# Input blocks of a hybrid decoder layer: both token tiles of the first and last unit side by side, and the gate weights one unit sooner

## The chip, the cores and the metric

The kernel is one program on 1 core of one Trainium2 chip. The metric is device microseconds (us) of one execution; lower is better. The engines are TensorE (PE; PEld is its weight load), VectorE (DVE), ScalarE (ACT), GpSimd (POOL) and SyncE (SP), which here issues nearly all DMAs, in order.

## The reference

One layer on 2048 tokens of width 1024, all in fp32:

```python
h = rmsnorm(x, norm_w)
u, z_s, q, k, v, z_a = split(h @ w_in)             # six blocks of 512 columns
y_s = s5_branch(u, ...)                            # complex diagonal state space, scan over tokens, half-GLU
y_s = y_s * silu(z_s)
y_a = diff_attention(rope(rmsnorm(q)), rope(rmsnorm(k)), v, ...)   # 4 heads, two maps each, causal
y_a = y_a * silu(z_a)
x = x + concat([y_s, y_a]) @ w_out
gate = sigmoid(x @ ple_w_gate)
x = x + gate * (p @ ple_w_proj)
```

## The kernel before

**Precision.** Each large product is made of three TensorE passes over operands split in a high and a low part (`passes`: high by high, high by low, low by high). In the trace the parts are `wh`/`wl` for weights and `xh`/`xl` for tokens. So a tile of 128 tokens by 512 columns takes 8 rows of weights (128 of the 1024 inputs each) by 3 passes, 24 matmuls into one PSUM bank.

**Stage 1, the input products** (to about 710 us). The 2048 tokens are two halves, and a half is four units of 256 tokens, t = 0 to 3, each of two tiles of 128 tokens, j = 0 and 1. `blocks` lists the work: u of the second half and of the first, then k, zs, v, q, za of the first half, then zs, k, v, q, za of the second. u and zs are made with the weights as the stationary operand (line 778, `pmm` in pieces of 256 tokens). q, k, v and za are made with the tokens as the stationary operand (line 824, `pmm` of 128 tokens by 512 columns): the code writes all 8 rows for j = 0 and then all 8 rows for j = 1.

The weights come through `Streamer` `ws`, a ring of 8 rows (`WB`). A row is one DMA of 256 KB into `wraw` (three such buffers, `WRB`), a scaled copy on ACT to `wh` (line 282) and the rest on DVE to `wl` (line 283). `ws.release()` gives back one row and has the next one loaded; it is called behind the last use of the row, so in the last unit of a block, behind the row's matmuls for j = 1. The next block needs its rows from its first unit on. `KOUT = (0, 3)` names the first and the last unit; for zs they are already written row by row (line 762).

A tile of q or k leaves PSUM through a chain: square on ACT (line 842), sums on DVE (844), three small steps on POOL (845 to 847), the scaling on DVE (850), which is the last reader of the bank, then rotation on DVE, four transposes on PE into `ptr` (865) and two reads of `ptr` (867, 868). `ps_mm`, the pool of `pmm`, has four banks.

Between the units, `background` puts in pieces of the state-space branch: tables and 32 groups one behind the other (lines 507 to 656, `U`, `tab`, `parg`, `na`, `zz`, `pss`), and the half-GLU (`g...`, lines 676 to 719). It uses all engines. The program's order is not that of the code: a scheduler with a time model of its own orders the instructions of each engine when the program is built, and each engine then runs its list in order.

**Stage 2, attention** (about 710 to 1158 us), 4 heads by 8 units, with the first half of the output product (`half`) put in between.

**Stage 3a, the second half of the output product** (to about 1234 us): eight units t = 0 to 7. A unit's result is added on DVE to `x1`. Units 0 to 2 (`EOP = 3`) use one PSUM bank, `pmf`, 12 matmuls at a time, each time added by line 1185; from t = 3 on there are seven more banks (`pm`, line 1189). In this stage `gate_w` also prepares the gate weights: for each of four row pairs k it loads two tiles `wgr` (line 1161, two buffers), forms seven sums and differences (line 1154, `wgt`) and splits each in high and low (ACT line 1149, POOL or DVE line 1150, `wg`). One `next(gw)` is half of a k. `GWS` says how many halves follow the code of unit t: `{3: 2, 4: 2, 5: 3, 6: 1}`. Ahead of each load POOL copies a column of the previous unit's `x1` into `wgr` (line 1160), so that the load cannot start before that unit is done.

**Stage 3b, the gate** (from about 1250 us to the end): seven products per pair of units (line 1262, `pg`), from `oph`/`opl`, made of `x1` by ACT and POOL (lines 1235, 1236), and `wg`; PLE products (1278), and the output.

Of the kernel before, what the change touches and what calls it, by code (L numbers as in the profile page):

```python
# [11 lines left out]
F32 = mybir.dt.float32  # L12
# [52 lines left out]
KOUT = (0, 3)  # L65
WB = 8
ACB = 3
EOP = 3
GWS = {3: 2, 4: 2, 5: 3, 6: 1}
XEB = 14  # L70
RA3 = 2
SSE = 0
# [46 lines left out]
def hymba_kernel(ctx, tc, x_t, p_t, positions, norm_w, w_in, lam_re, lam_im, log_dt, b_re, b_im,  # L119
# [3 lines left out]
    V, A, G, T = nc.vector, nc.scalar, nc.gpsimd, nc.tensor  # L123
# [74 lines left out]
    with ExitStack() as p1:  # L198
# [7 lines left out]
        ps_mm = p1.enter_context(tc.tile_pool(name="ps_mm", bufs=4, space=PSUM))  # L206
# [69 lines left out]
        def build_w(c0, k):  # L276
            def make():
                raw = pr.tile([128, 512], F32, name="wraw", bufs=WRB)
                nc.sync.dma_start(raw, win[k * 128:(k + 1) * 128, c0:c0 + 512])
                wh = pw.tile([128, 512], F32R, name="wh")  # L280
                wl = pw.tile([128, 512], F32R, name="wl")
                A.activation(wh, raw, AF.Copy, scale=nw[:, k:k + 1])  # L282
                V.scalar_tensor_tensor(wl, raw, nw[:, k:k + 1], wh.bitcast(F32), op0=ALU.mult, op1=ALU.subtract)  # L283
                return wh, wl
            return make
# [8 lines left out]
        ws = Streamer([build_w(c0, k) for _, _, c0 in blocks for k in range(8)], WB)  # L294
# [438 lines left out]
        passes = ((0, 0), (0, 1), (1, 0))  # L733
        ude = None
        xi = 0
        for bi, (hf, kind, c0) in enumerate(blocks):
            leaving = bi == len(blocks) - 1 or blocks[bi + 1][0] != hf
            for t in range(4):
                tok = hf * HALF + t * 256
                xt = xs.get(xi + t)  # L740
                last_t = t == 3
                if kind == "zs" and t == 0:
                    norm_cols(hf)
                if kind in ("u", "zs"):
                    if kind == "u" and t == 0:
                        ude = [pg1.tile([128, L, 128], F32, name="stg") for _ in range(4)]
                    if bi == 0 and t < 2:

                        if t == 0:
                            first = [pool.tile([128, 512], F32, name=nm)[:, :256] for pool, nm, n in  # L750
                                     ((ps_mm, "pmm", 4), (ps_ss, "pss", 3), (ps_tr, "ptr", 1)) for _ in range(n)]
                            for k in range(8):
                                w = ws.get(k)
                                for t_ in range(2):
                                    for cb in range(4):
                                        for n, (a_, b_) in enumerate(passes):
                                            T.matmul(first[t_ * 4 + cb], lhsT=w[b_][:, cb * 128:cb * 128 + 128],
                                                     rhs=xs.get(t_)[a_][:, k, :],
                                                     start=(k == 0 and n == 0), stop=(k == 7 and n == 2))
# [6 lines left out]
                    else:  # L766
                        pms = [ps_mm.tile([128, 512], F32, name="pmm") for _ in range(2)]
                        pos_ = [pms[cb // 2][:, (cb % 2) * 256:(cb % 2) * 256 + 256] for cb in range(4)]
                        order = [(cb, k) for cb in range(4) for k in range(8)]
                    for cb, k in order:  # L770
# [3 lines left out]
                        pm = pos_[cb]  # L774
                        w = ws.get(bi * 8 + k)
                        if bi > 0 or t > 1:
                            for n, (a_, b_) in enumerate(passes):
                                T.matmul(pm, lhsT=w[b_][:, cb * 128:cb * 128 + 128], rhs=xt[a_][:, k, :],  # L778
                                         start=(k == 0 and n == 0), stop=(k == 7 and n == 2))
# [34 lines left out]
                else:  # L814
                    if kind in ("q", "k"):
                        sh_ = pg1.tile([128, H, 256], F32R, name="stg")
                        sl_ = pg1.tile([128, H, 256], F32R, name="stg")
                    for j in range(2):
                        ti = (tok // 128) + j
                        pm = ps_mm.tile([128, 512], F32, name="pmm")  # L820
                        for k in range(8):
                            w = ws.get(bi * 8 + k)
                            for n, (a_, b_) in enumerate(passes):
                                T.matmul(pm, lhsT=xt[a_][:, k, j * 128:j * 128 + 128], rhs=w[b_],  # L824
                                         start=(k == 0 and n == 0), stop=(k == 7 and n == 2))
                            if last_t and j == 1:
                                ws.release()
                        rows = slice(ti * 128, ti * 128 + 128)
                        if kind == "v":
                            vo = pt.tile([128, 512], F32, name="t2")  # L830
# [103 lines left out]
    with ExitStack() as p2:  # L934
# [90 lines left out]
        for h in range(H):  # L1025
# [6 lines left out]
            for i in ORD[h]:  # L1032
# [6 lines left out]
                for qt in range(2):  # L1039
                    tq = slice(qt * 128, qt * 128 + 128)  # L1040
                    n = t0 + qt * 128 + 128
# [15 lines left out]
                    for ci, cl in enumerate(chunks):  # L1057
                        end = 640 if ci == len(chunks) - 1 else 512
                        pi, o = where[ci]
                        for m in range(2):  # L1060
                            pss = ps_s.tile([128, 512], F32, name="pss2")
                            for e in range(2):
                                T.matmul(pss[:, :cl], lhsT=qd[:, e, m, tq], rhs=ks[m][:, c0:c0 + cl],  # L1063
                                         start=e == 0, stop=e == 1)
# [26 lines left out]
                    for kg in range(0, len(blocks_), 4):  # L1091
# [6 lines left out]
                        for k in range(nk):  # L1098
                            T.matmul(po[:, 0:128], lhsT=wt[:, k, :], rhs=vt[:, kg + k, :],  # L1099
                                     start=kg + k == 0, stop=kg + k == len(blocks_) - 1)  # L1100
# [23 lines left out]
    with ExitStack() as p3:  # L1124
# [12 lines left out]
        with ExitStack() as p3a:  # L1137
# [38 lines left out]
            for t, i in enumerate(order):  # L1176
# [4 lines left out]
                for n0 in range(0, 8, 2):  # L1181
# [5 lines left out]
                    pm = ps3.tile([128, 2, 256], F32, name="pm3")  # L1187
# [4 lines left out]
                else:  # L1192
                    kept.append(x1)
                for _ in range(GWS.get(t, 0)):
                    next(gw)
# [200 lines left out]
```

## Time and profile before

| | us |
|---|---|
| median of 3 runs (lowest, highest) | 1471.44 (1465.84, 1471.6) |
| profiled execution, its own time | 1468.54 |
| span of the profiled execution | 1466.8 |
| PE busy in the span | 1389.2 (95%) |
| DVE busy | 1067.0 (73%) |
| ACT, POOL busy | 768.0 (52%), 522.4 (36%) |
| PE idle before its first gate product | 15.4 |

The span is what the profile shows of one execution; 1.7 us lie around it. A busy share is a mean over all stages. A row of the waits names who waited for whom, how long in all, how often and the longest. In a row of a timeline, `[3.98 <-DVE wl L283]` says that the engine was idle for 3.98 us before that instruction, and that DVE's `wl` of line 283 came last of what it waited for.

### The profile page before, as it was taken

To read this page: it belongs to the slowest core of one execution; us is meant where nothing else is said; L and a number is where in the kernel's file an instruction comes from. 1 tells how busy PE (TensorE), PEld (TensorE's weight loads), DVE (VectorE), ACT (ScalarE), POOL (GpSimd) and SP (SyncE) were. 2 spreads that over 40 slices of the span, in tenths; PEclk is the share of its full clock that TensorE was granted. 3 is DMA by queue.
4 is the path that set the end of the run, shared out by engine and by line. 5 is a ranking of instruction groups with operands and counts; after the bars stand their busy time and mean duration, and the time that the engine had idled before them with its cause. 6 is when DMAs were issued, how large, how long until landed. Compare 5 with 4: busy or idle time off the path is not lost.

```text
span 1466.8 us, 27419 instructions
## 1 busy us (share of the span) xinstructions
PE 1389.2 (95%) x9602; PEld 1279.5 (87%) x9602; DVE 1067.0 (73%) x2527; ACT 768.0 (52%) x1689; POOL 522.4 (36%) x670
## 2 busy tenths in 40 slices
PE   7999899999899999999899999999999996999998
PEld 7998798778698878888699999988989896899998
DVE  8568788789898866774687767767887248656754
ACT  8543335456554545553577677777787213332231
POOL 6632410043010411340255455544335334543440
PEclk9999899999999999999999999999999998899999
DMA  7448666546755287556854644644443455132221
GB/s 244 131 127 263 200 190 210 159 125 211 237 179 177 94 232 185 150 168 203 255 145 125 181 127 119 177 127 152 116 144 122 153 189 205 58 116 76 70 80 58
DMA packets 219410, 230.34 MB, mean 157 GB/s; under 512 B 62712, under 2 KB 168328, under 8 KB 216712
## 3 DMA queue, kind: packets, MB, share of 16 engines
q1 hardware_dynamic: 216968, 224.40, 49.8%
q10 hardware_dynamic: 2304, 4.20, 0.8%
q8 instruction: 75, 1.23, 0.3%
q14 instruction: 63, 0.52, 0.1%
HBM read 152.19 MB, written 84.72 MB: 162 GB/s over the span
## 4 chain that ended last, share of the span: by engine, by line
PE 48%; DVE 19%; DMA 15%; ACT 6%; issue 6%; POOL 5%; SPq 2%; ACTq 0%; DVEq 0%; POOLq 0%
PE pg L1262 11%; PE pmf L928 7%; PE po L1099 7%; PE pss L1063 7%; PE ptw L1095 3%; PE pl L1278 3%; DMA wraw<-in_w_in_dram 3%; PE pmm L824 2%; PE pss L707 2%; PE pmm L778 2%; POOL qst L846 2%; DMA tab_scr<-tx 2%; DVE wl L283 2%; PE pm L928 2%; DVE zz L644 1%
## 5 line engine op out<-in xcount | busy, mean ns | idle before, releaser
L824 PE MATMUL pmm<-wh,xh 128*128 128x512 f32 x512 | 197.6, 395 | 7.0 <-ACT wh L282 6.6
L824 PE MATMUL pmm<-wl,xh 128*128 128x512 f32 x512 | 200.8, 395 | 2.1 <-DVE wl L283 2.1
L824 PE MATMUL pmm<-wh,xl 128*128 128x512 f32 x512 | 200.2, 393 | 0.0
L1063 PE MATMUL pss<-ks,qd 128*128 128x512 f32 (+3 forms) x640 | 185.1, 387 | 7.5 <-DVE st L1065 4.0
L1074 ACT ACTIVATE s<-s,st 128x1024 f32<-128x1024 f32 (+4 forms) x192 | 171.5, 897 | 37.3 <-DVE st L1065 32.8
L1262 PE MATMUL pg<-oph,wg 128*128 128x256 f32 x896 | 164.1, 286 | 15.4 <-ACT oph L1235 15.4
L1262 PEld LDWEIGHTS pg<-oph,wg 128*128 128x128 f32 x896 | 141.6, 195 | 15.6 <-ACT oph L1235 15.6
L1099 PE MATMUL po<-vt,wt 128*128 128x128 f32 x1088 | 152.3, 276 | 2.9 <-ACT yo L1111 1.5
L1099 PEld LDWEIGHTS po<-vt,wt 128*128 128x128 f32 x1088 | 142.2, 192 | 11.2 <-ACT wt L1097 3.2
L1065 DVE CUSTOM_DVE_ANT_0 s<-pss,mk,st 128x512 f32<-128x512 f32 (+2 forms) x192 | 122.1, 651 | 23.3 <-PE pss L1063 21.7
L778 PE MATMUL pmm<-xh,wl 128*128 128x256 f32 x448 | 128.9, 291 | 4.1 <-DVE wl L283 4.1
L778 PE MATMUL pmm<-xh,wh 128*128 128x256 f32 x448 | 124.9, 294 | 6.0 <-DVE stg L788 3.2
L778 PE MATMUL pmm<-xl,wh 128*128 128x256 f32 x448 | 128.5, 290 | 0.0
L1262 PE MATMUL pg<-opl,wg 128*128 128x256 f32 x448 | 127.2, 285 | 0.3 <-POOL opl L1236 0.3
L824 PEld LDWEIGHTS pmm<-wh,xh 128*128 128x128 f32 x512 | 96.2, 189 | 27.6 <-ACT wh L282 8.7
L1063 PEld LDWEIGHTS pss<-ks,qd 128*128 128x128 f32 x640 | 100.8, 192 | 17.5 <-DVE st L1065 8.0
L824 PEld LDWEIGHTS pmm<-wl,xh 128*128 128x128 f32 x512 | 96.6, 189 | 21.1 <-DVE wl L283 3.0
L824 PEld LDWEIGHTS pmm<-wh,xl 128*128 128x128 f32 x512 | 96.7, 189 | 18.2
L928 PE MATMUL pmf<-yh,woh 128*128 128x256 f32 x352 | 105.0, 298 | 4.5 <-DVE x L1185 3.6
L596 POOL TENSOR_TENSOR U<-U,rl 128x256 f32<-128x256 f32 x32 | 28.3, 884 | 220.5 <-DMA U<-ug_scr 169.5
L1065 DVE CUSTOM_DVE_ANT_0 s<-pss,mk 128x512 f32<-128x512 f32 (+3 forms) x128 | 78.5, 629 | 31.2 <-PE pss L1063 26.7
L928 PE MATMUL pmf<-yl,woh 128*128 128x256 f32 x352 | 99.8, 284 | 0.0
(385 smaller groups left out, 3906.1 us busy)
## 6 DMA issues: line engine op xcount, KB each, us to landing
wraw<-in_w_in_dram SPq DMA_DIRECT2D x96, 256.0 KB
xraw<-in_x_t_dram SPq DMA_DIRECT2D x40, 256.0 KB
tab<-tab_scr SPq DMA_DIRECT2D x64, 136.0 KB
qd<-qh_scr SPq DMA_DIRECT2D x64, 128.0 KB
qd<-ql_scr SPq DMA_DIRECT2D x64, 128.0 KB
xr<-in_x_t_dram SPq DMA_DIRECT2D x32, 256.0 KB
yin<-yt_scr SPq DMA_DIRECT2D x16, 512.0 KB
xp_scr<-xp SPq DMA_DIRECT2D x32, 256.0 KB
```

What stands on the lines that cost most here:

```text
L283: V.scalar_tensor_tensor(wl, raw, nw[:, k:k + 1], wh.bitcast(F32), op0=ALU.mult, op1=ALU.subtract)
L707: T.matmul(pm[:, e, :], lhsT=a_[:, k, m * 128:m * 128 + 128], rhs=b_[k], start=(k == 0 and n == 0), stop=(k == 3 and n == 2))
L778: T.matmul(pm, lhsT=w[b_][:, cb * 128:cb * 128 + 128], rhs=xt[a_][:, k, :], start=(k == 0 and n == 0), stop=(k == 7 and n == 2))
L824: T.matmul(pm, lhsT=xt[a_][:, k, j * 128:j * 128 + 128], rhs=w[b_], start=(k == 0 and n == 0), stop=(k == 7 and n == 2))
L928: T.matmul(pm[:, e, :], lhsT=w[k][b_][:, ms], rhs=y[a_][:, k, :], start=(k == 0 and n == 0), stop=(k == 3 and n == 2))
L1063: T.matmul(pss[:, :cl], lhsT=qd[:, e, m, tq], rhs=ks[m][:, c0:c0 + cl], start=e == 0, stop=e == 1)
L1065: V.tensor_tensor_reduce(sr[m][pi][:, o:o + cl], pss[:, :cl], mk[:, end - cl:end], scale=1.0, scalar=3.4e38 if ci == 0 else st[:, 2 * ci - ...
L1074: A.activation(sr[m][pi][:, :cl], sr[m][pi][:, :cl], AF.Exp, bias=st[:, ci + m:ci + m + 1], scale=-1.0, accum_out=st[:, 12 + 2 * pi + m:13 ...
L1095: T.transpose(ptw[:, k, :], blocks_[kg + k], ident)
L1099: T.matmul(po[:, 0:128], lhsT=wt[:, k, :], rhs=vt[:, kg + k, :], start=kg + k == 0, stop=kg + k == len(blocks_) - 1)
L1262: T.matmul(banks[mp][:, e], lhsT=wg[n][k][b_][:, m * 128:m * 128 + 128], rhs=x_[a_][:, k], start=k == 0 and q == 0, stop=k == 3 and q == 2)
L1278: T.matmul(banks[mp][:, e], lhsT=wp[k][b_][:, m * 128:m * 128 + 128], rhs=p_[a_][:, k], start=(k == 0 and q == 0), stop=(k == 1 and q == 2))
```

## The change

Two edits. In blocks k, v, q and za the first and the last unit (`KOUT`) now take two banks at once and go through the weights row by row, three matmuls for j = 0 and three for j = 1 of each row; in the last unit the row is given back right behind these six. What follows a tile (its way out of PSUM) is the same code, behind both tiles. And `GWS` becomes `{2: 2, 3: 2, 4: 2, 5: 2}`: each k of the gate weights stands whole behind one unit, the first behind unit 2. The number of matmuls and of all other operations is the same.

```diff
-GWS = {3: 2, 4: 2, 5: 3, 6: 1}
+GWS = {2: 2, 3: 2, 4: 2, 5: 2}
...
+                    both = t in KOUT
+                    for j, k in [(j, k) for k in range(8) for j in range(2)] if both else []:
+                        if k == 0:
+                            pms = (pms if j else []) + [ps_mm.tile([128, 512], F32, name="pmm")]
+                        w = ws.get(bi * 8 + k)
+                        for n, (a_, b_) in enumerate(passes):
+                            T.matmul(pms[j], lhsT=xt[a_][:, k, j * 128:j * 128 + 128], rhs=w[b_],
+                                     start=(k == 0 and n == 0), stop=(k == 7 and n == 2))
+                        if last_t and j == 1:
+                            ws.release()
                     for j in range(2):
                         ti = (tok // 128) + j
-                        pm = ps_mm.tile([128, 512], F32, name="pmm")
-                        for k in range(8):
+                        pm = pms[j] if both else ps_mm.tile([128, 512], F32, name="pmm")
+                        for k in range(0 if both else 8):
                             w = ws.get(bi * 8 + k)
                             for n, (a_, b_) in enumerate(passes):
                                 T.matmul(pm, lhsT=xt[a_][:, k, j * 128:j * 128 + 128], rhs=w[b_],
                                          start=(k == 0 and n == 0), stop=(k == 7 and n == 2))
-                            if last_t and j == 1:
-                                ws.release()
```

The scheduler orders the whole program anew. Nine lines are added, so in the changed kernel line 824 is 825 (side by side) or 835, and every later line stands nine or so lower (1150 is 1159, 1154 is 1163, 1185 is 1194, 1189 is 1198).

On DVE, where the first half's block k ends and zs begins, this stood before (`na` and `tabt` are the state-space branch's, and read `parg`, which a DMA brings; `wl` are the first three rows of zs's weights):

```order
L643 MEMSET zz 128x1
L850 TENSOR_TENSOR t_2411<-pmm,qst 128x512
L868 SCALAR_TENSOR_TENSOR stg<-ptr,knw,stg 128x4x128
L858 TENSOR_TENSOR ra<-t_2411,kc 128x128
L539 TENSOR_TENSOR na<-parg 128x512
L541 TENSOR_TENSOR tabt<-parg 128x512
L859 TENSOR_TENSOR rb<-t_2411,ks 128x128
L844 TENSOR_REDUCE qst<-t_2564 128x8
L581 TENSOR_TENSOR tx<-pt_2055 128x544
L283 SCALAR_TENSOR_TENSOR wl<-wraw,nw,wh 128x512 x3
```

And now, at the same place:

```order
L643 MEMSET zz 128x1
L859 TENSOR_TENSOR t_2364<-pmm,qst 128x512
L853 TENSOR_REDUCE qst<-t_2404 128x8
L867 TENSOR_TENSOR ra<-t_2364,kc 128x128
L868 TENSOR_TENSOR rb<-t_2364,ks 128x128
L869 TENSOR_TENSOR t_2364<-ra,rb 128x8x8
L870 TENSOR_TENSOR t_2364<-ra,rb 128x8x8
L283 SCALAR_TENSOR_TENSOR wl<-wraw,nw,wh 128x512 x3
L539 TENSOR_TENSOR na<-parg 128x512
L541 TENSOR_TENSOR tabt<-parg 128x512
```

The three `wl` stood behind the two readers of `parg` and now stand ahead of them.

On PE, in the last unit of block k of the second half, rows of the weights are `wh_6322`, `wh_6334` and so on, and the two tiles are `pmm_7112` and `pmm_7159` before, the end of the first tile and the start of the second:

```order
L824 MATMUL pmm_7112<-wh_6412,xh_5442 128x512
L824 MATMUL pmm_7112<-wl_6413,xh_5442 128x512
L824 MATMUL pmm_7112<-wh_6412,xl_5443 128x512
L824 MATMUL pmm_7159<-wh_6322,xh_5442 128x512
L824 MATMUL pmm_7159<-wl_6323,xh_5442 128x512
L824 MATMUL pmm_7159<-wh_6322,xl_5443 128x512
L824 MATMUL pmm_7159<-wh_6334,xh_5442 128x512
```

Now the start of the unit, with the tiles `pmm_7112` and `pmm_7116`:

```order
L825 MATMUL pmm_7112<-wh_6322,xh_5442 128x512
L825 MATMUL pmm_7112<-wl_6323,xh_5442 128x512
L825 MATMUL pmm_7112<-wh_6322,xl_5443 128x512
L825 MATMUL pmm_7116<-wh_6322,xh_5442 128x512
L825 MATMUL pmm_7116<-wl_6323,xh_5442 128x512
L825 MATMUL pmm_7116<-wh_6322,xl_5443 128x512
L825 MATMUL pmm_7112<-wh_6334,xh_5442 128x512
```

Row 6322's last use came behind 27 matmuls of the unit and now comes behind 6; the last row's last use is the unit's last matmul in both.

On DVE in stage 3a, `x_14802` is unit 1's `x1`, `x_14915` unit 2's, `x_15028` unit 3's. Before:

```order
L1185 TENSOR_TENSOR x_14802<-x_14802,pmf 128x256 x4
L1185 TENSOR_TENSOR x_14915<-x_14915,pmf 128x256 x2
L1189 TENSOR_TENSOR x_15028<-x_15028,pm_15036 128x512
L1185 TENSOR_TENSOR x_14915<-x_14915,pmf 128x256
L1189 TENSOR_TENSOR x_15028<-x_15028,pm_15062 128x512
L1185 TENSOR_TENSOR x_14915<-x_14915,pmf 128x256
```

Now, with `x_15056` as unit 3's:

```order
L1194 TENSOR_TENSOR x_14802<-x_14802,pmf 128x256
L1194 TENSOR_TENSOR x_14915<-x_14915,pmf 128x256 x2
L1163 TENSOR_TENSOR wgt<-wgr 128x512
L1198 TENSOR_TENSOR x_15056<-x_15056,pm_15064 128x512
L1159 TENSOR_TENSOR wg_14651<-wgt,wg_14650 128x512
L1163 TENSOR_TENSOR wgt<-wgr,wgt 128x512
L1194 TENSOR_TENSOR x_14915<-x_14915,pmf 128x256
L1163 TENSOR_TENSOR wgt<-wgr,wgt 128x512
L1163 TENSOR_TENSOR wgt<-wgr 128x512
L1159 TENSOR_TENSOR wg_14665<-wgt,wg_14664 128x512
L1198 TENSOR_TENSOR x_15056<-x_15056,pm_15090 128x512
```

Five of the first k's DVE instructions, the first of which needs a DMA, now stand between unit 2's additions; all of them stood behind unit 2 before.

## Rows read from the trace of the kernel before

**Rows 1.** Stages: length, busy us (count) per engine, granted clock, DMA share, GB/s.
```profile
118.00:310.00 192.00, 182.13 (x1050) 159.36 (x1049) 158.93 (x423) 84.76 (x172) 37.92 (x47) 0.97 0.66 206
310.00:505.00 195.00, 185.63 (x1099) 162.05 (x1098) 173.88 (x396) 106.28 (x228) 48.66 (x56) 0.99 0.56 173
505.00:710.00 205.00, 199.96 (x1075) 170.01 (x1074) 132.80 (x303) 99.42 (x224) 45.71 (x56) 0.99 0.67 191
...
1130.00:1200.00 70.00, 66.44 (x546) 64.69 (x545) 20.69 (x55) 16.58 (x51) 19.64 (x37) 1.00 0.42 151
1200.00:1250.00 50.00, 34.67 (x289) 34.47 (x288) 43.34 (x47) 19.36 (x32) 25.74 (x20) 0.89 0.55 208
1250.00:1256.00 6.00, 5.67 (x24) 5.36 (x25) 2.90 (x1) 2.39 (x3) 5.95 (x3) 0.50 0.00 0
```
**Rows 2.** Waits of PE, whole span: us in total, times, longest.
```profile
PE pg L1262 <- ACT oph L1235: 15.4, 1, 15.4
PE pmm L824 <- ACT wh L282: 6.6, 3, 3.5
```
**Rows 3.** Timeline of PE at the block boundaries: start, us, what, idle before.
```profile
168.48 0.58 PE L778 MATMUL pmm<-xh,wl 128*128 128x256 f32 x1 [3.98 <-DVE wl L283]
...
287.13 0.50 PE L824 MATMUL pmm<-wl,xh 128*128 128x512 f32 x1 [1.92 <-DVE wl L283]
...
294.63 0.73 PE L824 MATMUL pmm<-wh,xh 128*128 128x512 f32 x2 [1.17 <-ACT wh L282]
...
400.68 0.62 PE L778 MATMUL pmm<-xh,wh 128*128 128x256 f32 x3 [2.03 <-ACT wh L282]
...
469.06 0.97 PE L824 MATMUL pmm<-wh,xh 128*128 128x512 f32 x3 [3.49 <-ACT wh L282]
...
525.46 0.75 PE L824 MATMUL pmm<-wh,xh 128*128 128x512 f32 x1 [1.97 <-ACT wh L282]
```
**Rows 4.** Windows of PE alone behind three of these: busy, clock, DMA, GB/s.
```profile
170.00:180.00 10.00, 10.00 (x59) 0.63 0.88 271
400.00:410.00 10.00, 8.84 (x57) 0.83 0.63 201
...
520.00:530.00 10.00, 8.03 (x31) 0.83 0.79 258
```
**Rows 5.** Timeline of DVE at the first of these boundaries.
```profile
164.51 0.69 DVE L539 TENSOR_TENSOR na<-parg 128x512 f32<-128x512 f32 x1 [1.61 <-DMA parg<-par_scr]
...
167.68 2.07 DVE L283 SCALAR_TENSOR_TENSOR wl<-wraw,nw,wh 128x512 fp32r<-128x512 f32 x3
```
**Rows 6.** Chain of waits, a stretch of stage 1: start, us, what.
```profile
596.26 8.65 PE pmm L824 x38
```
**Rows 7.** Timelines of ACT and DVE, block k: one tile's way out.
```profile
154.48 0.69 ACT L842 ACTIVATE t<-pmm,rstd 128x512 f32<-128x512 f32 x1 [2.46 <-DVE qst L844]
...
161.35 0.69 DVE L850 TENSOR_TENSOR t<-pmm,qst 128x512 f32<-128x512 f32 x1
```
**Rows 8.** Timelines of DVE and SP: last additions of units 1 and 2, first gate load.
```profile
1164.83 0.42 DVE L1185 TENSOR_TENSOR x<-x,pmf 128x256 f32<-128x256 f32 x1 [1.78 <-PE pmf L928]
...
1192.35 0.42 DVE L1185 TENSOR_TENSOR x<-x,pmf 128x256 f32<-128x256 f32 x1 [0.87 <-PE pmf L928]
...
1193.21 1.34 SPq L1161 DMA_DIRECT2D wgr<-in_ple_w_gate_dram  x2
```
**Rows 9.** Instructions of lines 1154 and 928: ns min/median/max, first and last start.
```profile
L1154 DVE TENSOR_TENSOR wgt<-wgr,wgt x8: 678/1598/2914, 1201.6 to 1244.0; 128x512 f32<-128x512 f32 x8
...
L928 PE MATMUL pm<-yl,woh x160: 279/283/283, 1169.2 to 1234.4; 128*128 128x256 f32 x160
```
**Rows 10.** Timelines of DVE, ACT and PE: third and last gate rows, first gate product.
```profile
1234.54 1.28 DVE L1150 TENSOR_TENSOR wg<-wgt,wg 128x512 fp32r<-128x512 f32 x2
...
1248.93 1.99 ACT L1235 CAST oph<-x 128x1024 fp32r<-128x1024 f32 x2 [2.98 <-DVE wg L1150]
...
1250.03 2.17 PE L1262 MATMUL pg<-oph,wg 128*128 128x256 f32 x8 [15.36 <-ACT oph L1235]
```

## The prediction

> **What bounds the kernel now.** I read the windows by stage first. In the three windows of stage 1 PE is busy 182.13 of 192, 185.63 of 195 and 199.96 of 205 us [rows 1]; the idle rest is 9.87 + 9.37 + 5.04 = 24.3 us, and that is all that an edit of stage 1 can win by closing gaps. DVE is busy 83% and 89% of the first two of these windows [rows 1]: it is the runner-up, and whatever is given to it sooner is taken from something else. At the end of stage 3a PE does 34.67 us of work in 50 [rows 1], while it did 66.44 in the 70 before.
>
> The waits of PE come second. One is large and stands alone: 15.4 us, once, before the first gate product, ended by ACT's `oph` [rows 2]. On the rows of the weights (ACT's `wh`) PE waits 6.6 us in three places [rows 2]. The timeline of PE at the block boundaries names those and three that DVE's `wl` or a late `wh` ends: k to zs 3.98, v to q 1.92 and 1.17, za to zs 2.03, zs to k 3.49, k to v 1.97 [rows 3], together 14.56 us. Behind three of them the granted clock of a 10 us window falls to 0.63, 0.83, 0.83 [rows 4], that is part of the time at half speed: 3.7 + 1.7 + 1.7 = 7.1 us more if that clock is what the waits bring about. Waits and clock of the boundaries make 21.7 us.
>
> The chain of waits comes third. Where nothing is missing it runs through PE alone, 38 matmuls in 8.65 us, 0.228 us each [rows 6]; a tile of 24 is 5.46 us and the two tiles of a unit 10.9 us.
>
> **The gate weights.** Removed: nothing; all the loads, sums and splits stay. Moved: each k of the four. A load of k waits for the `x1` of the unit before, and the first one is issued at 1193.21, behind unit 2's last addition at 1192.35 [rows 8]. Now the first load waits for unit 1, whose last addition is at 1164.83 [rows 8], 27.5 us sooner. The second load waits for unit 2, as the first did, so the second, third and fourth k stand where the first, second and third stood. That shift is what I price: in the trace before, the third k's last split starts at 1234.54 and two take 1.28 us [rows 10], so all gate weights would be there at 1235.8. `oph` starts at 1248.93, and the idle time ahead of it on ACT was ended by DVE's `wg` [rows 10]: it stands behind the preparation. What is late next is PE itself: the last output projection starts at 1234.4 [rows 9], and `x1` of the last units follows it. With `oph` at 1235.9 and the first product 1.1 us behind it, as now (1250.03 against 1248.93 [rows 10]), the product comes at 1237.0: 13.0 us sooner.
>
> Its price: on DVE five instructions of the first k now stand between unit 2's additions, which the order shows, and `pmf` is a single bank, so PE's next 12 matmuls for unit 2 wait for the addition ahead of them. The first sum waits for its load: before it started at 1201.6 [rows 9], 8.4 us behind the issue at 1193.21 [rows 8]. Issued at about 1165.7, the data are there at 1174.1. Between two of unit 2's additions stand then two sums of 1.6 us (the median [rows 9]), a split of 0.64 and an addition of 0.42, 4.3 us: the third addition at 1178.4, the fourth at 1183.1, and before the last one was at 1192.35. By that nothing is late. If the third addition is already due when the sum starts to wait, PE could lose up to the whole 8.4 us. I take 2.3, nearer to the first. So 13.0 - 2.3 = 10.7. Behind the wait the clock is 0.50 in the 6 us that follow [rows 1]: 24 matmuls in 5.67 us, of which half, at most 2.8, are lost. A wait of 2.4 us instead of 15.4 may leave the clock up, but 2.98 us of idle DVE and ACT time stand just there too [rows 10], so I take 1.0, a third. The gate term: -11.7. Its ends: 0 (the wait is only put elsewhere: DVE has 43.34 us of work in the last 50 [rows 1]) and -17 (the whole 15.4 and half of the clock).
>
> Stage 3b begins with the product and all of it hangs on that start, so I carry the term to the end undiminished.
>
> **The blocks.** Removed: nothing; the same matmuls, ways out and loads. Moved: in the last unit of k, v, q and za a row of weights is given back behind 6, 12, ... 48 of the unit's matmuls and not behind 27, 30, ... 48. The first row is free 21 matmuls, 4.8 us, sooner, the fourth 12 matmuls or 2.7, the last not at all [rows 6]. In the first unit the rows are wanted 6 matmuls or 1.4 us apart instead of 0.7. Each row is a DMA, then `wh` on ACT, then `wl` on DVE, so the next block's first rows can be there up to 4.8 us sooner if SP, ACT and DVE take them at once. Each boundary by itself:
> - k to zs, 3.98 us [rows 3]: `wl` stood on DVE behind a reader of `parg` that waits 1.61 us for its DMA, and its first three start at 167.68 [rows 5]. The order now has the three `wl` ahead of that reader. With the 3.7 of the clock [rows 4] 7.7; I take 7.
> - v to q, 1.92 + 1.17: v's rows come free sooner, the second wait is for the next ones; I take 2.
> - za to zs, 2.03 and 1.7 of the clock: za's rows come free sooner; I take 3.
> - zs to k, 3.49: zs was written row by row already, and its releases are where they were. Only k's slower use in its first unit helps; I take 1.
> - k to v, 1.97 and 1.7 of the clock; I take 3.
>
> Together 16 of 21.7. Not all of it comes home. The state-space pieces are pushed behind the rows on DVE, which is 83% and 89% busy [rows 1], and the chain that they form must end with stage 1. I take half: -8. Its ends are -20, nearly all that the boundaries hold, and +5, where the two tiles' ways out fall together and are not covered.
>
> **That price of side by side**, for both tiles end within three matmuls of each other and want DVE, ACT and POOL at once. One tile's way out holds its bank from 154.48 to 161.35 + 0.69, 7.56 us [rows 7]. Before, the second tile ended 5.46 us behind the first. Now both are full together, and if the second follows at half that time the pair is out after some 11.4 us. The next unit takes the two other banks of four, and the unit behind it wants the pair 10.9 us later. The cover is the other two banks, and it is short by half a microsecond on this estimate, so it can decide either way; none of PE's large waits before is for `pmm`'s bank [rows 2]. The Trainium skill, in "Perfetto Trace Analysis", section Matmuls, asks that independent groups of matmuls rotate through PSUM banks, so that one is evacuated beside the next group's matmuls; tile after tile does that, side by side does it only by pairs. By that rule alone the blocks' edit would be a loss, which is the third rival below; no wait on a bank in the trace before bears it out.
>
> **Sum.** The profiled execution took 1468.54 us (its span and 1.7 around it), 2.9 below the median of the runs, 1471.44, and 2.7 above the lowest. 1468.54 - 11.7 - 8 = 1448.8; against the median the same terms give 1451.7. I name 1450.
>
> **Rivals.**
> 1. Only the gate counts; the boundaries' gain is used up on DVE. For it: DVE's 83% and 89%, and that both tiles' ways out now come in a burst. Against it: five of the six waits are for weights and not for the state-space chain. 1468.54 - 11.7 = 1457.
> 2. The boundaries give all: -11.7 - 21.7 makes 1435. For it: three of them pull the clock down [rows 4]. Against it: zs to k isn't touched.
> 3. Slower: banks. q and k have a first and a last unit in each half, eight such units. If each makes PE wait for the first tile's bank by the second tile's share of the way out, 3.8 us (half of 7.56), that is 30 us: 1468.54 + 30 - 11.7 = 1487. It decides from 1.5 us a unit on, where eight eat the gate's term. Against it: four banks, and the scheduler can put other work of PE there.
> 4. The gate brings nothing: the wait is replaced by one on DVE's sums between unit 2's additions, or `oph` waits for the last unit's `x1`. Only the blocks count: 1460.5.
>
> **Chances.** Forecast .55, with a range of its own of 1441 to 1457 (the gate term from -8 to -15, the blocks from -4 to -13); rival 1 .25, rival 2 .10, rival 3 .05, rival 4 .05. The range 1437 to 1464 takes in rivals 1 and 4 and leaves out most of 2 and all of 3, and the least that both terms may give. A measurement of this kernel tells 0.5%, 7 us, from no change. Faster by more than that: .86 (all of the forecast and rival 2, most of 1 and 4); within it .09 (rivals 1 and 4 with the gate term at its small end); slower .05 (rival 3).
>
> **What would show it.** Gate: the first load at about 1166 by the old clock of the trace; the four k evenly spread; PE's wait before the first product below 3 us and the window behind it above 0.50; no wait of PE for `pmf` above 3 us. It is wrong if `oph` still waits for `wg`, or PE waits for unit 2's additions by 8 us. Blocks: the 3.98 at k to zs gone and its window's clock near 1; the waits at za to zs and k to v gone; the 3.49 at zs to k still there, about 2.5. PE's idle time in the three windows of stage 1 falls from 24.3 to about 13 us. PE waits ended by DVE's scaling of `t` (the bank's last reader) would prove rival 3; equal idle time in stage 1 at other places would prove rival 1. The forecast fails as a whole if stage 1 ends later than before.

## The result and the profile after

The changed kernel takes 1485.83 us (median of 4 runs, 1479.07 to 1489.09), the kernel before 1469.65 beside it: a ratio of 1.0108 (95% interval 1.0072 to 1.0144). It is 16 us slower. 1450 was forecast, with a range to 1464.

The profiled execution has a span of 1484.0 us, 17.2 more than before. Three instants on PE split it: the last input product (709.97 before, 716.99 now), the first product into `pm`, with which unit 3 of the output product begins (1166.83 and 1194.74), and the first gate product (1250.03 and 1265.65).

| us | before | changed | difference |
|---|---|---|---|
| start to the last input product | 710.0 | 717.0 | +7.0 |
| from there to the first `pm` product ("attention" below) | 456.9 | 477.7 | +20.9 |
| from there to the first gate product | 83.2 | 70.9 | -12.3 |
| from there to the end | 216.8 | 218.4 | +1.6 |

The gate gives what was forecast, and attention, which the prediction carried at nothing, loses more than that. The table is of one execution each; how far stage 1 varies stands below. The windows that answer to [rows 1], with all of attention and the 6 us around the first gate product behind them (length, busy us and count per engine, granted clock, DMA share, GB/s):

```profile
118.00:310.00 192.00, 181.19 (x1043) 158.10 (x1042) 159.13 (x430) 86.10 (x175) 41.84 (x49) 0.97 0.68 207
310.00:505.00 195.00, 184.76 (x1078) 158.81 (x1077) 169.67 (x386) 103.11 (x222) 51.22 (x52) 0.99 0.56 170
505.00:710.00 205.00, 197.18 (x1065) 167.88 (x1064) 128.83 (x300) 97.94 (x223) 49.15 (x59) 0.99 0.63 175
717.00:1194.70 477.70, 446.43 (x3299) 412.86 (x3298) 339.19 (x956) 336.01 (x832) 210.23 (x384) 0.98 0.48 141
...
1265.00:1271.00 6.00, 3.49 (x17) 3.12 (x18) 5.97 (x4) 3.02 (x4) 5.36 (x2) 0.68 0.00 1
```

PE's idle time in the three windows of stage 1 is 28.9 us, not 13 as forecast; it was 24.3. PE's waits from 118 us to the end of stage 1 show why. The kernel before:

```profile
PE pmm L824 <- ACT wh L282: 6.6, 3, 3.5
PE pmm L778 <- DVE wl L283: 4.1, 2, 4.0
PE pmm L824 <- DVE wl L283: 2.1, 2, 1.9
PE pmm L778 <- ACT wh L282: 2.0, 1, 2.0
PE pss L530 <- DVE wal L525: 1.8, 2, 1.2
PE pss L530 <- ACT ysb L652: 1.3, 3, 0.7
```

And the changed kernel (line 874 is the transposes of q and k, into the single bank of `ptr`, and 877 is DVE's reading of it; 530 is the state-space branch):

```profile
PE ptr L874 <- DVE stg L877: 6.8, 5, 2.6
PE pss L530 <- ACT xah L524: 4.4, 5, 1.9
PE pss L530 <- DVE wal L525: 2.5, 3, 1.4
PE pss L530 <- ACT ysb L652: 2.3, 3, 1.8
PE pmm L778 <- ACT wh L282: 2.3, 2, 2.1
PE pss L530 <- ACT mgh L524: 2.3, 2, 1.2
PE pmm L778 <- DVE t L859: 1.0, 1, 1.0
...
PE pmm L778 <- DVE wl L283: 0.9, 2, 0.7
...
PE pmm L825 <- DVE wl L283: 0.4, 2, 0.2
...
PE pmm L825 <- ACT wh L282: 0.2, 1, 0.2
```

The waits for rows of the weights fall from 14.8 to 3.8 us: the edit does what it says. All others together rise from 8.9 to 24.3, on the transposes of the two tiles, which now come in a burst, and on the state-space pieces.

### The profile page after: what moved, and what is told of

It reads as the page before. It is cut to its first block, busy times and chain, and to the rows that moved or that the text cites. A ratio compares the mean times of both kernels' runs of the same rounds, so it can differ in the third digit from the quotient of the medians.

```text
span 1484.0 us, 27412 instructions
## 1 busy us (share of the span) xinstructions
PE 1399.1 (94%) x9602; PEld 1283.9 (87%) x9602; DVE 1063.1 (72%) x2527; ACT 769.7 (52%) x1689; POOL 526.4 (35%) x670
## 4 chain that ended last, share of the span: by engine, by line
PE 45%; DMA 18%; DVE 17%; POOL 7%; issue 6%; ACT 6%; SPq 2%; DVEq 0%; ACTq 0%; POOLq 0%
PE pg L1271 11%; PE po L1108 6%; PE pmf L937 6%; PE pss L1072 6%; PE pl L1287 3%; PE ptw L1104 3%; DMA wraw<-in_w_in_dram 3%; PE pmm L825 3%; POOL qst L855 2%; DMA yin<-yt_scr 2%; DMA xraw<-in_x_t_dram 2%; PE pmm L778 2%; ACT s L1083 2%; PE pm L937 2%; PE pss L707 1%
## 5 line engine op out<-in xcount | busy, mean ns | idle before, releaser
L1072 PE MATMUL pss<-ks,qd 128*128 128x512 f32 (+3 forms) x640 | 188.6, 393 | 13.5 <-issue 3.8
L778 PE MATMUL pmm<-xh,wh 128*128 128x256 f32 x448 | 128.9, 295 | 6.0 <-ACT wh L282 2.6
L835 PE MATMUL pmm<-wh,xh 128*128 128x512 f32 x256 | 101.0, 395 | 0.5 <-DVE s_ta L415 0.5
L596 POOL TENSOR_TENSOR U<-U,rl 128x256 f32<-128x256 f32 x32 | 32.8, 1025 | 190.5 <-DMA U<-ug_scr 153.1
L937 PE MATMUL pmf<-yh,wol 128*128 128x256 f32 x352 | 100.0, 284 | 0.0
```

Of the source, the lines that this page charges most:

```text
L596: UE.tensor_tensor(U, U, rl, op=ALU.mult)
L937: T.matmul(pm[:, e, :], lhsT=w[k][b_][:, ms], rhs=y[a_][:, k, :], start=(k == 0 and n == 0), stop=(k == 3 and n == 2))
```

## The experiments

Fifteen further kernels ran, e1 to e15. The length of attention is that of the table above, from one profiled execution each; a ratio is to the kernel before on the same chip, with its 95% interval. Not all ran on one chip, and the kernel before takes 1465.5 to 1469.7 us (medians) on those used.

| run | side by side in | gate | ratio | attention, us |
|---|---|---|---|---|
| before | none | old | 1 | 456.9 |
| changed | all 16 units | new | 1.0108 (1.0072 to 1.0144) | 477.7 |
| e1_gate_only | none | new | 0.9921 (0.9903 to 0.9940) | 457.2 |
| e2_blocks_only | all 16 | old | 1.0141 (1.0117 to 1.0164) | 477.4 |
| e3_first_unit | 8 first units | new | 0.9948 (0.9928 to 0.9968) | 458.4 |
| e4_q_k_only | 8 of q and k | new | 1.0094 (1.0077 to 1.0111) | 474.3 |
| e5_one_unit_za1 | last of za, first half | new | 1.0009 (0.9992 to 1.0025) | 468.5 |
| e6_last_k_v_half2 | last of k and v, second half | new | 0.9936 (0.9913 to 0.9960) | 458.9 |
| e7_last_za_half2 | last of za, second half | new | 0.9940 (0.9920 to 0.9960) | 458.4 |
| e8_one_unit_k1 | first of k, first half | new | 0.9949 (0.9931 to 0.9968) | 459.6 |
| e9_13_of_16 | all but 3 last units of k, q, q | new | 0.9920 (0.9898 to 0.9942) | 455.8 |
| e10_15_of_16 | all but first of q, first half | new | 1.0099 (1.0065 to 1.0133) | 477.2 |
| e11_last_q_half2 | last of q, second half | new | 0.9908 (0.9877 to 0.9939) | 454.0 |
| e12_all_but_last_q_half2 | all but last of q, second half | new | 1.0013 (0.9995 to 1.0031) | 464.9 |
| e13_fill, e14_ord, e15_flag | all 16, attention's order drawn anew | new | 1.0062, 1.0078, 1.0037 | 472.2, 475.2, 470.6 |

PE's list of attention, compared matmul by matmul without buffer numbers, is the same in before, e1 and e6 (2746 matmuls), and in e3 behind four more score products. Another list is the same in the changed kernel and e2 (2753), and e4 has 2741 of its matmuls in that order. A third is the same in e7 and e9. Before and the changed kernel have 918 matmuls in the same order, a third. (The trace counts more, since it shows most products into `po` twice.)

### The two parts apart

e1 is the kernel before with one line changed; e2 is the changed kernel with that line put back:

```diff
-GWS = {3: 2, 4: 2, 5: 3, 6: 1}
+GWS = {2: 2, 3: 2, 4: 2, 5: 2}
```

> Only the four numbers of GWS are changed; the blocks are written as before, so stage 1 and attention keep the order that they had. Theory A (the gate's part works as predicted, and what is lost is lost in stage 1 and in attention by the blocks' part): PE's wait before the first gate product falls from 15.4 to about 3 us and the time by 11 to 13 us, to 0.992 of before. Theory B (the earlier gate loads cost in stage 3a or attention what they save): the wait is gone but the time is within 3 us of before, 0.998 to 1.002.

> Only the blocks' part; GWS as before, so the 15 us wait of PE before the first gate product should stay. Theory A: 26 to 30 us slower than before, ratio 1.018 to 1.021: some 7 us at the end of stage 1 and some 19 us in attention and the output product, with attention in the order of the changed kernel. Theory B: the loss of the changed kernel alone, about 16 us, ratio 1.011, since the gate's part gives nothing.

e1 came out as theory A has it: 0.9921, 11.6 us faster than 1465.47. The blocks alone cost 1.0141, 21 us, less than the 26 to 30 expected, for the 7 us of stage 1 are not there. Stage 1 ends at 705.3 in e2 and at 717.0 in the changed kernel, though PE's 3965 matmuls up to there are the same; e13 to e15, which have that order too, end it at 712.5, 709.8 and 711.6. It ends at 704.6 in e1 and at 710.0 before, with the same 3972 matmuls. So stage 1 differs by 5 to 12 us between executions of one order, and what the blocks do to it can't be told from one trace of each. Attention repeats: 477.7 and 477.4 in the one order, 456.9 and 457.2 in the other. The lost time is there.

Before, PE's longest wait in attention behind its first 30 us is this one (start, us, what, idle before):

```profile
1089.24 1.16 PE L1099 MATMUL po<-vt,wt 128*128 128x128 f32 x8 [1.20 <-ACT wt L1097]
```

The four longest waits of e2 stand at the same places in the changed kernel, where three of them are the longest. The changed kernel:

```profile
720.68 1.28 PE L1072 MATMUL pss<-ks,qd 128*128 128x512 f32 x3 [3.31 <-DMA qd<-ql_scr]
...
737.10 0.39 PE L937 MATMUL pmf<-yh,woh 128*128 128x256 f32 x1 [1.23 <-ACT yh L923]
...
847.09 0.51 PE L1072 MATMUL pss<-ks,qd 128*128 128x512 f32 x1 [3.85 <-issue]
...
1146.13 0.80 PE L1108 MATMUL po<-vt,wt 128*128 128x128 f32 x2 [3.92 <-ACT wt L1106]
```

And e2, where stage 1 ended 11.7 us sooner:

```profile
707.86 0.93 PE L1072 MATMUL pss<-ks,qd 128*128 128x512 f32 x3 [2.15 <-DMA qd<-ql_scr]
725.35 0.39 PE L937 MATMUL pmf<-yh,woh 128*128 128x256 f32 x1 [2.38 <-ACT yh L923]
835.58 1.19 PE L1072 MATMUL pss<-ks,qd 128*128 128x512 f32 x2 [3.70 <-issue]
1134.08 0.80 PE L1108 MATMUL po<-vt,wt 128*128 128x128 f32 x2 [4.08 <-ACT wt L1106]
```

Take 11.7 from the first list and each wait stands within 1.2 us of the second. They belong to the order.

### Which units

From here to e12 a unit written tile after tile in its block's last place gives its rows back as before. Only the condition differs:

```diff
-                    both = t in KOUT
+                    both = t == 0                              # e3
+                    both = t in KOUT and kind in ("q", "k")    # e4
```

> Both parts, but side by side in the first unit of a block only; the last unit is written tile after tile and gives its rows back as before. The scheduler then puts attention in the order that it has before. Theory A1 (attention's 19 us come from the new order of attention): attention as long as before, the time 1455 to 1462, ratio 0.990 to 0.995. Theory A2 (the bunched ways out of the tiles cost in stage 1 and the delay is carried on, whatever attention's order): four of the eight q and k units are still side by side, so half of the 26 us stay and the time is about 1470, ratio 0.998 to 1.002.

> Both parts, but side by side in the blocks q and k only; v and za tile after tile. The scheduler then puts attention in the order of the changed kernel. Theory A1: attention is as long as in the changed kernel, so 17 to 21 us over before there; the time 1478 to 1488, ratio 1.006 to 1.012, whatever stage 1 does by a few us. Theory A2: all eight units with a long way out are still side by side, and the time is that of the changed kernel too; the two theories part on run e3_first_unit, here only by where the time is lost: A1 behind the end of stage 1, A2 ahead of it.

Both went as A1 has it: the order of before comes with 458.4 us and 0.9948, nearly the order of the changed kernel with 474.3 and 1.0094. But e3 and e4 differ in the units too, so single units followed:

```diff
+                    both = last_t and bi == 6          # e5: za, first half
+                    both = last_t and bi in (8, 9)     # e6: k, v, second half
+                    both = last_t and bi == 11         # e7: za, second half
+                    both = t == 0 and bi == 2          # e8: k, first half
```

> The gate's part, and side by side in one single unit: the last of block za of the first half, at about 395 us, over 300 us ahead of attention. All other units tile after tile. The scheduler then puts attention in a third order, neither that of before nor of the changed kernel. Theory A1 (attention's order decides, and any change ahead can draw another one): attention has another length than the 457 us from the last input product to the first product of unit 3 that it had three times in the order of before; by how much can't be said, the order of before is the one that the kernel was tuned on, so I expect 5 to 20 us more: 1459 to 1474, ratio 0.996 to 1.006. Theory A3 (side by side in the last units near attention leaves its first heads short of something): no such unit here, attention 457 us and the time that of the gate's part alone, 1454, ratio 0.992.

> The gate's part, and side by side in the last units of blocks k and v of the second half; all others tile after tile. Attention keeps the order of before. Theory A1: attention 457 us as with the gate's part alone, and the wait at k to v (1.97 us and 1.7 of the clock) goes: 0 to 4 us below the gate's part alone, 1450 to 1454, ratio 0.989 to 0.992. Theory A3: two of the last units are side by side, and attention grows by some 5 to 10 us: ratio 0.996 to 0.999.

> The gate's part, and side by side in the last unit of za of the second half alone, the last unit ahead of attention. A fourth order of attention. Theory A1: another length of attention, by my guess 5 to 20 us over 457, 1459 to 1474. Theory A3: this is the unit next to attention, whose two banks come free together and later, so attention loses most of the 20 us: about 1470, with the loss in its first 20 us; by A1 the loss is spread over attention.

> The gate's part, and side by side in one single unit, the first of block k of the first half, at about 120 us, 590 us ahead of attention. A fifth order of attention. Theory A1: another length of attention than 457 us, by my guess 5 to 20 us more, 1459 to 1474, ratio 0.996 to 1.006. Theory A3: attention 457 us, time 1454, ratio 0.992.

Theory A3 falls: e7 is side by side in the unit next to attention and loses nothing. e5 is side by side in one unit, over 300 us ahead, and attention is 11 us longer. e6 had the order of before and its length; its ratio, 0.9936, misses the 0.989 to 0.992 expected and is no better than e1's, so the gain of two boundaries can't be seen. My guess of 5 to 20 us for any new order was wrong for e7 and e8, whose orders are new and only 1.5 and 2.7 us longer.

```diff
+                    both = t in KOUT and (kind in ("v", "za") or t == 0 or bi == 8)   # e9
+                    both = t in KOUT and (bi, t) != (5, 0)                            # e10
```

> Both parts, side by side in 13 of the 16 units: all but the last units of k of the first half and of q of both halves, which are tile after tile. The scheduler then puts attention in the order of run e7_last_za_half2, where it took 458 us. Theory A1 (attention's order decides): attention 457 to 460 us and the time 1454 to 1462, ratio 0.990 to 0.996, some 25 us below the changed kernel, though nearly all of its units are as there. Rival A2 (side by side itself costs, unit by unit): 13 of 16 units, 9 of 12 without the last ones of v and za, so most of the 25 us stay: 1472 to 1482, ratio 1.003 to 1.009.

> Both parts, side by side in 15 of the 16 units, all but the first unit of q of the first half, at about 330 us. The scheduler then puts attention in nearly the order of run e5_one_unit_za1, where it took 468.5 us. Theory A1: attention 467 to 471 us, the time 1464 to 1472, ratio 0.997 to 1.003, as with one unit side by side. Rival A2: as the changed kernel, attention 475 to 478 us, ratio 1.009 to 1.012.

e9 is the strongest of them: 13 of 16 units side by side, attention 455.8 us, 0.9920. Side by side in itself does not cost the 20 us. e10 was a miss for A1, and its numbers are those of A2, which e9 has just ruled out: PE has 2735 of e5's 2750 matmuls in their order, and yet takes 477.2 us and not 468.5. So there is something besides PE's order.

### What attention begins with

Of the long kernels so far all but e5 have the last unit of q of the second half side by side, and no short one has:

```diff
+                    both = last_t and bi == 10                  # e11
+                    both = t in KOUT and (bi, t) != (10, 3)     # e12
```

> The gate's part, and side by side in the last unit of q of the second half alone. This unit is side by side in every run with a long attention but e5_one_unit_za1 (468.5 us), and tile after tile in every run with a short one. Theory A4 (this unit is the cause: its queries are the last that attention needs, and come out late in a burst): attention 465 to 478 us, the time 1462 to 1475, ratio 0.995 to 1.004, the loss in the first 30 us. Theory A1 (the order that the scheduler draws): a sixth order, 80% like that of before; attention 457 to 465 us, 1454 to 1462, ratio 0.990 to 0.996.

> Both parts, side by side in 15 of the 16 units, all but the last unit of q of the second half. Attention's order is 85% like that of the changed kernel. Theory A4: attention 456 to 463 us and the time 1453 to 1462, ratio 0.990 to 0.996. Theory A1: attention mostly as in the changed kernel, 468 to 478 us, 1466 to 1480, ratio 0.999 to 1.008.

Neither theory holds as it stood. That unit alone (e11) costs nothing: 454.0 us, the shortest of all and below A1's range. Leaving it out (e12) takes 12.9 of the 20.9 us away and leaves 8; its 464.9 lies between the two ranges. What the unit does in company is seen on SP, which stores q (`ql_scr<-stg`), loads the queries (`qd`) and later the output product's first input (`yin<-yt_scr`). Before, where stage 1 ends at 710.0:

```profile
676.71 0.38 SPq L872 DMA_DIRECT2D ql_scr<-stg  x1
...
696.87 1.78 SPq L1020 DMA_DIRECT2D qd<-ql_scr  x2
...
713.27 0.38 SPq L913 DMA_DIRECT2D yin<-yt_scr  x1
```

And in the changed kernel, where it ends at 717.0:

```profile
690.19 0.36 SPq L881 DMA_DIRECT2D ql_scr<-stg  x1
...
711.44 0.60 SPq L1029 DMA_DIRECT2D qd<-ql_scr  x1
...
732.10 0.41 SPq L922 DMA_DIRECT2D yin<-yt_scr  x1
```

Seen from the end of stage 1, the last q is stored 26.8 us ahead and not 33.3, the queries are loaded 5.6 us ahead and not 13.1, and `yin` 15.1 us behind and not 3.3. The three score products of 512 columns that wait for the queries ran 7.2 us ahead of the end before (702.76) and run 3.7 us behind it now (720.68 above). The first 30 us of attention and the rest, before:

```profile
710.00:740.00 30.00, 25.20 (x149) 21.54 (x148) 24.96 (x55) 22.07 (x48) 13.13 (x18) 0.89 0.76 217
740.00:1166.83 426.83, 414.62 (x3145) 386.85 (x3144) 308.98 (x894) 309.32 (x781) 201.03 (x365) 1.00 0.46 138
```

The changed kernel:

```profile
717.00:747.00 30.00, 21.21 (x103) 15.40 (x102) 23.66 (x53) 20.71 (x38) 7.20 (x10) 0.89 0.94 261
747.00:1194.74 447.74, 425.26 (x3199) 397.50 (x3198) 315.53 (x905) 315.30 (x795) 203.07 (x374) 0.99 0.45 133
```

e5, with a good start and a poor order:

```profile
710.30:740.30 30.00, 25.12 (x145) 20.67 (x144) 24.67 (x61) 21.82 (x46) 11.11 (x18) 0.89 0.74 217
740.30:1178.78 438.48, 419.58 (x3153) 392.75 (x3153) 310.36 (x890) 310.56 (x782) 203.55 (x367) 0.99 0.46 134
```

Before, 149 matmuls run in the first 30 us; now 103, and 54 more stand in the rest (seven score products that ran ahead of the end of stage 1 before now run behind it). The rest is 20.9 us longer: 10.6 of it is more busy time (54 matmuls at the rest's mean of 0.132 us are 7.1; the remainder goes with a clock of 0.99 and not 1.00), 10.3 is more idle time (22.5 against 12.2). In e5 the start is as before, and its rest has 18.9 us idle: a poor order with a good start is 11.6 us longer than before.

e10 has PE's order of e5, all but 15 of its 2750 matmuls, and the last unit of q side by side in company:

```profile
708.80:738.80 30.00, 20.57 (x97) 15.98 (x96) 21.55 (x51) 18.01 (x37) 10.40 (x13) 0.83 0.77 220
738.80:1186.05 447.25, 428.06 (x3206) 400.31 (x3204) 316.82 (x906) 315.92 (x794) 205.43 (x371) 0.98 0.45 133
...
722.92 0.58 PE L939 MATMUL pmf<-yh,woh 128*128 128x256 f32 x1 [3.74 <-ACT yh L925]
```

Its rest idles as e5's does (19.2 and 18.9 us), but its first 30 us hold 97 matmuls and not 145. Counted from the end of stage 1, e10 is 6.9 us behind e5 when a tenth of the score products is done, and 8.7 when attention ends. So with nearly one order on PE a poor start makes attention 8.7 us longer. The seven kernels with that unit side by side among others (changed, e2, e4, e10, e13 to e15) have 85 to 111 matmuls in the first 30 us, the ten others 129 to 152.

Late queries are only a part of the poor start. Of the 46 matmuls fewer, 31 belong to the output product (22 against 53); score products are 37 and 38. The output product's first matmul comes 20.1 us behind the end of stage 1 (737.10 above) and not 9.4, behind the late `yin`, and it has moved back in PE's list too. In these 30 us of e10 PE does not wait for queries at all, but 3.74 us for `yh`, which ACT makes of `yin`; in e5 it waits 0.97 us there. Nor is it that the DMA engines are full: their share in these 30 us is 0.94 in the changed kernel, but 0.77 in e10, as before (0.76).

### Attention's order drawn anew

Stage 1 of these three is matmul for matmul that of the changed kernel on PE; one setting of attention differs:

```diff
-FILL = [2] * 4 + [1] * 28
+FILL = [2] * 5 + [1] * 27                       # e13
-ORD = [(0, 7, 1, 6, 2, 5, 3, 4), ...
+ORD = [(0, 7, 1, 5, 2, 6, 3, 4), ...            # e14
-FLAG = 0
+FLAG = -100                                     # e15
```

> The changed kernel with all 16 units side by side; one number is changed inside attention: FILL = [2] * 5 + [1] * 27, one more piece of the output product in attention's fifth unit. PE's list of stage 1 is row for row that of the changed kernel, and attention is in another order (1508 of PE's 2752 rows stand as there). Theory A1 (the length comes from the order of attention itself): a length of its own, not the 474 to 478 us of the changed kernel's order; of seven orders so far five gave 454 to 469, so I expect 455 to 470, and 1462 to 1477 us. Theory A5 (the side-by-side units of stage 1 leave attention something, late transfers or full queues, whatever its order): 474 to 478 us again, 1479 to 1486.

> The changed kernel, and in attention's first head two units change places (5 before 6). Stage 1 row for row as in the changed kernel; 1108 of PE's 2752 rows of attention stand as there. Theory A1: a length of its own, 455 to 470 us, the time 1462 to 1477. Theory A5: 474 to 478 us.

> The changed kernel with FLAG = -100, the priority that the scheduler gives the pieces of the output product inside attention. Stage 1 row for row as in the changed kernel; 1035 of PE's 2752 rows of attention stand as there. Theory A1: a length of its own, 455 to 475 us, the time 1462 to 1480. Theory A5: 474 to 478 us.

No theory takes all three: e14 lies in A5's range, e15 in the wider one that A1 gave it, e13 in neither. The length changes with the order (472.2, 475.2, 470.6), but none comes near 457. e13 in the same two windows:

```profile
712.50:742.50 30.00, 19.45 (x85) 14.46 (x84) 20.33 (x47) 18.23 (x33) 6.94 (x10) 0.83 0.91 241
742.50:1184.68 442.18, 427.34 (x3216) 399.42 (x3215) 315.42 (x909) 317.50 (x800) 206.40 (x374) 0.99 0.46 135
```

Its rest has 14.8 us idle, close to before's 12.2: this order has put most of the later waits right. The start is no better than the changed kernel's, 85 matmuls, and that is not mended. So both causes are there, of about equal size: the poor start, which comes out of stage 1 (8.7 us between e10 and e5), and the waits of the order (11.6 us between e5 and before).

The version to keep is the gate's part, alone (e1, 0.9921) or with side by side in the last unit of q (e11, 0.9908) or in 13 units (e9, 0.9920). Their intervals overlap, and all are faster than both kernels.

## Why the prediction was wrong

**Gate: right, its closeness in part luck.** Forecast -11.7; e1 measured 0.9921, -11.6. The wait before the first gate product fell from 15.36 [rows 10] to 2.57 in e1:

```profile
1233.06 2.14 PE L1262 MATMUL pg<-oph,wg 128*128 128x256 f32 x8 [2.57 <-ACT oph L1235]
```

That is 12.8, where 13.0 was worked out. The price was sized at 2.3 and is smaller, 0.8: in e1 unit 2's last addition comes 28.35 us behind unit 1's (1188.17 and 1159.82), in [rows 8] 27.52:

```profile
1159.82 0.42 DVE L1185 TENSOR_TENSOR x<-x,pmf 128x256 f32<-128x256 f32 x1 [1.78 <-PE pmf L928]
...
1188.17 0.42 DVE L1185 TENSOR_TENSOR x<-x,pmf 128x256 f32<-128x256 f32 x1 [0.87 <-PE pmf L928]
```

The 1.0 us of clock did not come in e1, where the 6 us behind the start show 0.50 as before:

```profile
1233.00:1239.00 6.00, 4.78 (x20) 4.50 (x21) 5.97 (x3) 2.48 (x3) 5.95 (x2) 0.50 0.00 0
```

In the changed kernel 0.68 stands there (1265 to 1271 above). The two errors, 1.5 one way and 1.0 the other, nearly cancel: the stretch from the first `pm` product to the first gate product is 71.2 us in e1 and 83.2 before, 12.0 less.

**Boundaries: right in mechanism.** Row waits were to lose most of 14.56; they lost 11.0. The rows of PE that answer to [rows 3], at k to zs, za to zs and zs to k (line 825, which has v to q, zs to k and k to v, has 0.4 and 0.2 us left in all):

```profile
168.13 0.80 PE L778 MATMUL pmm<-xh,wh 128*128 128x256 f32 x2 [2.11 <-ACT wh L282]
...
411.95 0.39 PE L778 MATMUL pmm<-xh,wl 128*128 128x256 f32 x1 [0.69 <-DVE wl L283]
...
475.16 0.74 PE L825 MATMUL pmm<-wh,xh 128*128 128x512 f32 x2 [0.19 <-ACT wh L282]
```

And those of DVE that answer to [rows 5]:

```profile
161.32 2.07 DVE L283 SCALAR_TENSOR_TENSOR wl<-wraw,nw,wh 128x512 fp32r<-128x512 f32 x3
163.30 0.69 DVE L539 TENSOR_TENSOR na<-parg 128x512 f32<-128x512 f32 x1
```

The three `wl` run ahead of `na` as the order said, and the wait at k to zs is halved, not gone as forecast; the granted clock from 170 to 180 us is 0.75, where it was 0.63 [rows 4]. I expected zs to k to stay at 2.5; it is 0.19.

**Given back: too little.** I took half, -8. The other waits, on the transposes and the state-space pieces above all, took all of it and more (8.9 to 24.3), and PE's idle time in stage 1 rose by 4.6 us: rival 1. What that is in time can't be told, since stage 1 varies by more than that.

**The step that failed** is "Sum": it adds the gate and the boundaries to the profiled time and carries the 457 us of attention between them at nothing, without a reason. The whole program was ordered anew, 918 of PE's 2746 matmuls of attention kept their order, and the prediction read the new order only at the three places of the edit. The runs showed 20.9 us there, of two kinds. One is a poor start: with q's last unit side by side among others, q is stored 6.5 us later against the end of stage 1, the loads that attention begins with come later, and so do the matmuls of its first 30 us. I had put the price of side by side, 3.8 us, on the second tile's way out and let it be decided by whether a bank is late; waits on the reader of `pmm` are 1.0 us in all. The other is that a new order has other waits, 10.3 us of idle time here.

Rival 3 had the sign, but not the place; it priced eight units at a bank. That its 1487 lies beside the measured 1485.83 is luck. By the Trainium skill's rule that groups of matmuls should rotate through banks ("Perfetto Trace Analysis", Matmuls) the loss would stand on `pmm`. The trace does not agree: it shows 1.0 us there, and 6.8 us on `ptr`, the single bank of the transposes, which I had not looked at. Those 6.8 us are waits of stage 1 and no part of the 20.9 us of attention.

**Not settled:** why q is stored later when its last unit is side by side in company, while alone (e11) it is stored 30.4 us ahead of the end at no cost. In the changed kernel its last transposes run some 29 us ahead of the end of stage 1, before some 36, and PE is not idle ahead of them in either, so it is their place in PE's list that moved; why the scheduler moves them is open. Open too is how much of the poor start is late loads and how much is the list itself, and which matmuls of an order make its waits. The 8.7 us of e10 against e5 are of e5's order; for the changed kernel's own, the halves, 10.6 and 10.3, are read from windows.

## What to carry to other kernels

Where a scheduler orders the whole program, compare the new list with the old one in every stage, far behind the edit too, before pricing a stage at nothing: the same instructions of attention took from 454 to 478 us here. Where an edit makes two results ready together, ask who reads them next and when, not only what holds them. Test the parts of a change apart first: one of these two was worth 0.8%, and the other hid it.

## What the runs showed that I had not expected

- Stage 1 in one and the same order of PE ended at 710.0 and 704.6 us, and in another at 717.0, 705.3, 712.5, 709.8 and 711.6; attention in one and the same order repeated within 3 us (456.9, 457.2, 458.4, 458.9; 477.7 and 477.4; 458.4 and 455.8).
- One unit written in another order at 395 us made attention, from 710 us on, 11 us longer (e5); with that unit and 12 others side by side it took 455.8 (e9).
- The wait of 3.85 us that the trace calls "issue" at 847.09 is at the same place put down to DVE in e4 (4.64, `st`), so what it really waits for is open.
